# Two-layer block in fp32: lo parts of the attention's weights and of finished head-pair rows on Pool, and the second pair's rotations issued one per tick behind the urgent VectorE work

## The chip, the core and the metric

The kernel runs on one core of one Trainium2 chip. A core has a matrix engine (TensorE, "PE" in the profile, with its weight loads shown apart as "PEld"), a vector engine (VectorE, "DVE"), an activation engine (ScalarE, "ACT"), a general engine (GpSimd, "POOL") and an engine that issues DMA transfers (SyncE, "SP"). The metric is the device time of one execution in microseconds, as a median over runs.

## The reference, cut to what matters

The reference is a two-layer block on a [1, 1024, 1024] input in fp32. Layer 0 mixes by a gated MLP and a convolution, layer 1 by attention; each layer ends in a convolutional FFN, and a norm closes the whole. The change lies in the attention of layer 1, which is in short:

```python
h = rms_norm(x, odd_norm_g[j])
qkv = (h @ odd_w_qkv[j]).reshape(bn, s, 3, ATTN_HEADS, HEAD_DIM)   # 16 heads of 64
q = rotary(qkv[:, :, 0], pos)        # x1*cos - x2*sin, x2*cos + x1*sin
k = rotary(qkv[:, :, 1], pos)
v = qkv[:, :, 2]
o = dilated_attention(q, k, v)       # three (window, dilation) patterns,
                                     # merged by their log-sum-exps
x = x + o.reshape(bn, s, D_MODEL) @ odd_w_o[j]
```

## The kernel before, in words

**Exact products from two parts.** Every matrix operand is held as two fp32r numbers, a hi part and a lo part. The hi part is a cast, made by ACT (`hi_of`, L206 in the profile). The lo part is the original less its hi part, a subtraction (`lo_of`). All subtractions, additions and products of DVE and POOL go through one small recording class, so that in the profile they have one line, L138; they are told apart by engine and tile names. A projection is then three products (hi·hi, lo·hi, hi·lo; L268 to L270).

**The attention's stages.** The 16 heads are worked on as eight pairs, `hp` 0 to 7, each about 60 us long. In a pair there are 20 steps, each of two ticks. A step makes, on PE: the scores of a later query block (`pss`, L1482 and L1483), the transposes of exponentials made before (`ppt`, L1549 and L1550, in `turn`), and the product of transposed exponentials with the values (`po`, L1569, in `value`) for the step two steps back. Between PE's parts stand, for the scores, a masked maximum on DVE and an exponential on ACT; and, for the transposes, a cast to hi on ACT (tile `tt`), a subtraction to lo on DVE (tile `tt`, from `ppt` in PSUM), and on some steps a small POOL memset of the tile's unused corner.

**What is fed in between.** While one pair runs its steps, the next pair is prepared: `prepare(hp)` projects the keys (`rk`), the queries (`rq`) and the values (`rv`) of that pair, a unit at a time by `feed`. Each projection of keys or queries is then rotated (`rotate`): four SP transfers swap the halves of each head into a tile `sw` (L1352), DVE multiplies `sw` by the sine and `rk`/`rq` by the cosine and adds them, ACT casts the sum to a hi part `rh`, and DVE subtracts it to a lo part `rl`. SP transfers (L1378) then put hi and lo of one head into the stacked operands `k` and `st`. The ticks at which these five steps come are written in `ROTATE = (1, 6, 7, 8, 9, 10)`: swap 1 tick after the projection's end, the sine product after 6, and so on to the lo part after 10; the first pair, which has no steps to run beside it, uses `ROTATE_FIRST`.

**The weights.** `Weights` fetches [128 x 1024] weight rows ahead (SP, L231), casts hi on ACT, and one tick later (`lo_at`) subtracts for lo, on DVE unless `lo_eng` says otherwise. When the lo part is written, the next fetch is issued.

**The end of a pair.** `finish_pair` takes the reciprocal of the row sums, writes it to DRAM and reads it back broadcast over partitions (tile `r`), multiplies the output `o` by it on DVE, casts to hi on ACT (into `r`), and, `O_LOW` = 3 ticks after the product (8 in pair 6), subtracts for lo on DVE into `o`; two SP transfers bring both to DRAM (L1619). The output projection takes them from there: `O_GROUPS = ((0,1,2),(3,4),(5,6,7))`. The first group's projection is fed in between the steps of pair 7; it needs the residual rows `x`, which SP loads (L1651) when pair 7 has been prepared.

**What sets the order.** Each engine executes its instructions in program order. The program order is written by a ticker: `after(n, fn, late)` puts a function on the tick n ticks ahead, where functions are sorted by `late` (negative first); `tick()` runs those due now, and then the ticker's hooks. An instruction that waits for a transfer or for another engine therefore holds up everything that was written after it for its engine.

Of the kernel before, what the change touches and what calls it, by code (L numbers as in the profile page):

```python
# [12 lines left out]
F32R = mybir.dt.float32r  # L13
# [132 lines left out]
def block_kernel(ctx, tc, io, out):  # L146
# [58 lines left out]
    def hi_of(hi, src):  # L205
        nc.scalar.copy(hi, src)  # L206
# [1110 lines left out]
    def attention(x_dram, hT, then, late):  # L1317
# [4 lines left out]
        nc.gpsimd.dma_start(cos, io["cos"])  # L1322
        nc.gpsimd.dma_start(sin, io["sin"])
        sets = {}

        def project(raws, fins):
            ws = weights.take(4)
# [14 lines left out]
                return box[0]  # L1342
            return get

        def rotate(raw, fin_h, fin_l, at):
            st = {}

            def swap():
                st["sw"] = sw = stile(name="sw")
                for b in range(4):  # L1350
                    a = b ^ 1
                    nc.sync.dma_start(sw[32 * b:32 * b + 32, :],  # L1352
                                        raw()[32 * a:32 * a + 32, :])

            def m2():
                vec.tensor_tensor(st["sw"], st["sw"], sin, op=ALU.mult)

            def m1():
                vec.tensor_tensor(raw(), raw(), cos, op=ALU.mult)

            def add():
                vec.tensor_tensor(raw(), raw(), st["sw"], op=ALU.add)

            def hi():
                st["rh"] = stile(dt=F32R, name="rh")
                hi_of(st["rh"], raw())

            def lo():
                st["rl"] = stile(dt=F32R, name="rl")
                lo_of(st["rl"], raw(), st["rh"])  # L1370

            for n, fn in zip(at, (swap, m2, m1, add, hi, lo)):
                after(n, fn)
            after(at[-2] + 1, lambda: fin_h(st["rh"]), 1)
            after(at[-1] + 1, lambda: fin_l(st["rl"]))

        def stack(t, z, src, e):
            nc.sync.dma_start(f32v(t[z * HD:(z + 1) * HD, :]), f32v(src[e * HD:(e + 1) * HD, :]))  # L1378
# [1 line left out]
        def prepare(hp):  # L1380
# [51 lines left out]

            rk, rq, rv = lazy("rk"), lazy("rq"), lazy("rv")
            at = ROTATE if hp else ROTATE_FIRST
            fins = [lambda: rotate(rk, k_hi, k_lo, at), lambda: rotate(rq, q_hi, q_lo, at)]
            if hp:
                yield from project([rk], fins[:1])
                yield from project([rq], fins[1:])
# [145 lines left out]
        def finish_pair(hp):  # L1584

            o = outs_o.pop(hp)
            ls = lsum[hp]
            st = {}

            def a():  # L1590
                vec.reciprocal(ls, ls)

            def b():
                st["ps"] = bank("psl")
                nc.tensor.transpose(st["ps"][0:16, 0:P], ls, ident)

            def c():
                st["row"] = smpool.tile([16, P], F32, tag="lrow", name=nm("lrow"), bufs=1)
                nc.scalar.copy(st["row"], st["ps"][0:16, 0:P])
                nc.sync.dma_start(l_dram[hp], st["row"])  # L1600

            def d():
                st["r"] = r = stile(name="r")
                for e in range(2):
                    src = l_dram[hp, 8 * e:8 * e + 8, :].rearrange("a b -> (a b)")
                    nc.sync.dma_start(r[e * HD:(e + 1) * HD, :], src.partition_broadcast(HD))

            def f():
                vec.tensor_tensor(o, o, st["r"], op=ALU.mult)
                if hp == KT - 1:  # L1610
                    oh, ol = hpair([P, S], "o")
                    split(o, oh, ol)
                    o_acts[hp] = tok_view(oh, ol)
                    return

                def low():
                    lo_of(o.bitcast(F32R), o, st["r"])
                    for z, part in enumerate((st["r"], o)):
                        nc.sync.dma_start(o_dram[hp, z], part)  # L1619
                after(1, lambda: hi_of(st["r"].bitcast(F32R), o))  # L1620
                after(O_LOW if hp < KT - 2 else O_LOW_LAST, low)
            after(1, a)
            after(2, b)
            after(3, c)
            after(4, d)
            after(9, f)
# [13 lines left out]
        def all_units():  # L1640
            for hp in range(KT - 1):
                yield from prepare(hp)

            for n, _ in enumerate(prepare(KT - 1)):
                if 20 <= n < 20 + len(O_GROUPS[0]):
                    o_fetch(n - 20)
                yield
            xb = [htile([P, 2, D], F32, "x") for _ in range(2)]
            for i in range(NT):
                xs.append(xb[i // 2][:, i % 2, :] if i < 4 else stile(name="x"))  # L1650
                after(1, lambda i=i: nc.sync.dma_start(xs[i], x_dram[i * P:(i + 1) * P, :]))  # L1651
            while any(k not in o_acts for k in O_GROUPS[0]):
                yield "wait"
            yield from down_units([o_acts[k] for k in O_GROUPS[0]], weights.take(4, W_O_DELAY), xs)

        fill = all_units()
# [46 lines left out]
        for n, ks in enumerate(O_GROUPS[1:]):  # L1703
            tk.until(lambda: all(k in o_acts for k in ks))
            if ks is O_GROUPS[-1]:
                late()
            down_group([o_acts[k] for k in ks], weights.take(4), xs if n == 0 else xn,
                       then(xn) if ks is O_GROUPS[-1] else None, to=xn)
# [212 lines left out]
```

## Time and profile before

| | |
|---|---|
| median of 3 runs | 2214.24 us (2212.09, 2214.24, 2214.68) |
| the profiled execution's own time | 2212.54 us |
| its span in the profile | 2210.8 us |
| PE busy | 2174.6 us, 98% |
| DVE busy | 1618.0 us, 73% |
| ACT busy | 1096.3 us, 50% |
| POOL busy | 687.8 us, 31% |
| mean granted PE clock | 0.998 |

Times in the trace count from the span's start. The attention's projections and its eight pairs lie between about 1000 and 1520 us. A row of the timeline gives start, duration, engine, line, operation and tiles (output <- inputs), and, in brackets, the idle time before it and what ended that. A row of waits for PEld gives the total time that weight loads of that line waited for the named releaser, how often, and the longest. "PEld" waits are what delays PE in this kernel, since each product needs its weights first. The columns of a table by stretch are busy time and count of each engine in that stretch, then the granted PE clock, the DMA share and GB/s.

### The profile page before, as it was taken

To read this page: it belongs to the slowest core of one execution; us is meant where nothing else is said; L and a number is where in the kernel's file an instruction comes from. 1 tells how busy PE (TensorE), PEld (TensorE's weight loads), DVE (VectorE), ACT (ScalarE), POOL (GpSimd) and SP (SyncE) were. 2 spreads that over 40 slices of the span, in tenths; PEclk is the share of its full clock that TensorE was granted. 3 is DMA by queue.
4 is the path that set the end of the run, shared out by engine and by line. 5 is a ranking of instruction groups with operands and counts; after the bars stand their busy time and mean duration, and the time that the engine had idled before them with its cause. 6 is when DMAs were issued, how large, how long until landed. Compare 5 with 4: busy or idle time off the path is not lost.

```text
span 2210.8 us, 29238 instructions
## 1 busy us (share of the span) xinstructions
PE 2174.6 (98%) x10448; PEld 1819.9 (82%) x10448; DVE 1618.0 (73%) x2583; ACT 1096.3 (50%) x1667; POOL 687.8 (31%) x529
## 2 busy tenths in 40 slices
PE   6999999999999999999999999999999999999998
PEld 6888888888888888888888888888888888888886
DVE  6998769877777865555777777786797777778556
ACT  5345365444444445353556555554654444444532
POOL 1122033766666340040000000001466666653001
PEclk9999999999999999999999999999999999999999
DMA  5479422444434597356344545743234444349933
GB/s 184 105 149 181 168 86 72 146 164 157 171 138 168 181 365 285 141 181 155 92 113 118 134 118 131 215 167 107 77 124 163 166 157 172 136 159 347 362 133 116
DMA packets 140849, 359.47 MB, mean 163 GB/s; under 512 B 16672, under 2 KB 17056, under 8 KB 140704
## 3 DMA queue, kind: packets, MB, share of 16 engines
q1 hardware_dynamic: 134512, 335.15, 45.0%
q0 software_dynamic: 5040, 18.27, 4.4%
q10 hardware_dynamic: 1152, 4.19, 0.5%
q8 instruction: 82, 1.34, 0.2%
q14 instruction: 63, 0.52, 0.1%
HBM read 219.68 MB, written 104.31 MB: 147 GB/s over the span
## 4 chain that ended last, share of the span: by engine, by line
PE 79%; issue 9%; DVE 6%; ACT 2%; DMA 1%; POOL 1%; SPq 1%; DVEq 0%; POOLq 0%; ACTq 0%
PE psd L1261 10%; PE psb L1082 7%; PE psb L1085 7%; PE psb L1083 7%; PE psu L269 6%; PE psu L270 6%; PE psu L268 6%; PE psc L1083 3%; PE psc L1082 3%; PE psc L1085 3%; PE po L1569 3%; PE psa L1083 2%; PE psa L1082 2%; PE psa L1085 2%; PE psd L268 2%
## 5 line engine op out<-in xcount | busy, mean ns | idle before, releaser
L1261 PE MATMUL psd<-ab 128*128 128x512 f32 x1800 | 409.9, 389 | 0.0
L1261 PEld LDWEIGHTS psd<-ab 128*128 128x128 f32 x1800 | 337.6, 188 | 69.9
L268 PE MATMUL psu<-hTh,w 128*128 128x512 f32 (+1 forms) x592 | 236.4, 399 | 0.1
L270 PE MATMUL psu<-hTh,w 128*128 128x512 f32 (+1 forms) x592 | 229.0, 387 | 0.0
L269 PE MATMUL psu<-hTl,w 128*128 128x512 f32 (+1 forms) x592 | 228.7, 386 | 0.2 <-DVE hTl L138 0.2
L206 ACT CAST ab<-ab 128x1024 fp32r<-128x1024 f32 x150 | 156.0, 1051 | 139.3 <-PE psd L1261 52.6
L138 DVE TENSOR_TENSOR ab<-ab,ab 128x1024 fp32r<-128x1024 f32 x150 | 191.5, 1331 | 36.2 <-ACT ab L206 35.7
L138 DVE TENSOR_TENSOR x<-psd,x 128x512 f32<-128x512 f32 x152 | 101.7, 687 | 135.2 <-PE psd L1261 107.4
L138 POOL MEMSET tt<- 128x256 f32 x64 | 19.9, 312 | 490.1 <-PE ppt L1550 158.6
L138 POOL TENSOR_TENSOR y<-y,y 128x512 f32<-128x512 f32 x66 | 94.6, 1434 | 186.3 <-DMA act<-y 110.4
L1119 ACT COPY sn<-psb 128x512 f32<-128x512 f32 x120 | 70.4, 587 | 165.1 <-PE psb L1085 121.7
L206 ACT CAST tt<-ppt 128x512 fp32r<-128x512 f32 (+1 forms) x160 | 86.6, 542 | 102.6 <-PE ppt L1550 66.5
L138 DVE TENSOR_TENSOR tt<-ppt,tt 128x512 fp32r<-128x512 f32 (+1 forms) x160 | 101.2, 634 | 48.4 <-ACT tt L206 47.3
L270 PEld LDWEIGHTS psu<-hTh,w 128*128 128x128 f32 x592 | 111.8, 189 | 23.1
L269 PEld LDWEIGHTS psu<-hTl,w 128*128 128x128 f32 x592 | 112.3, 190 | 17.4 <-DVE hTl L138 0.6
L268 PEld LDWEIGHTS psu<-hTh,w 128*128 128x128 f32 x592 | 112.2, 190 | 17.2 <-ACT rv L1331 0.4
L138 POOL TENSOR_TENSOR sm<-sm,mhalf 128x1 f32<-128x1 f32 (+2 forms) x38 | 31.5, 829 | 293.8 <-DVE sm L138 293.8
L138 POOL TENSOR_TENSOR s<-wr 128x512 f32<-128x512 f32 x40 | 86.2, 2156 | 108.3 <-DVE psa L138 97.9
L1499 ACT ACTIVATE p<-p,sma 128x896 f32<-128x896 f32 (+7 forms) x128 | 99.5, 778 | 37.0 <-DVE sma L138 36.4
L138 DVE TENSOR_TENSOR wl<-wr,wh 128x1024 fp32r<-128x1024 f32 x88 | 117.3, 1333 | 0.5 <-ACT wh L206 0.5
L1569 PE MATMUL po<-tt,v 128*128 128x256 f32 x640 | 110.0, 292 | 5.2 <-DVE tt L138 4.9
L138 DVE TENSOR_TENSOR pse<-psc,sn 128x512 f32<-128x512 f32 x40 | 28.0, 699 | 117.9 <-ACT sn L1119 117.9
(251 smaller groups left out, 5845.2 us busy)
## 6 DMA issues: line engine op xcount, KB each, us to landing
wr<-in_w_up_dram SPq DMA_DIRECT2D x88, 512.0 KB, 4.3
ab<-act SPq DMA_DIRECT2D x154, 256.0 KB, 5.4
act<-y SPq DMA_DIRECT2D x66, 512.0 KB, 3.0
wq<-in_w_down_dram SPq DMA_DIRECT2D x44, 512.0 KB, 5.2
wt<-wq SPq DMA_DIRECT2D x44, 512.0 KB, 4.6
ab<-wt SPq DMA_DIRECT2D x88, 256.0 KB, 5.4
ab<-in_w_down_dram SPq DMA_DIRECT2D x66, 256.0 KB, 5.6
wr<-in_w_qkv_dram SPq DMA_DIRECT2D x24, 512.0 KB, 4.1
```

What stands on the lines that cost most here:

```text
L138: return fn(*args, **kw)
L206: nc.scalar.copy(hi, src)
L268: nc.tensor.matmul(out_ap, st[0], mv[0], start=first, stop=False)
L269: nc.tensor.matmul(out_ap, st[0], mv[1], start=False, stop=False)
L270: nc.tensor.matmul(out_ap, st[1], mv[0], start=False, stop=last)
L1082: nc.tensor.matmul(ps, st[0], mv[0], start=f, stop=False, skip_group_check=True)
L1083: nc.tensor.matmul(ps, st[0], mv[1], start=False, stop=False, skip_group_check=True)
L1085: nc.tensor.matmul(ps, st[1], mv[0], start=False, stop=e, skip_group_check=True)
L1119: nc.scalar.copy(self.sn[key], self.b)
L1261: nc.tensor.matmul(ps, a[:, c], b[:, HALF:D], start=first and k == 0, stop=last and k == 2, skip_group_check=True)
L1499: nc.scalar.activation(p, p, AF.Exp, bias=sm[:, 2:3], scale=0.125, accum_out=lsum[hp][:, c:c + 1])
L1569: nc.tensor.matmul(po[:, c], v2[:, kb, :], tt[:, z, 256 * n:256 * n + 256], start=(g == 0 and n == 0 and z == 0), stop=(g == j and n == 1 ...
```

## The change

Three things are written otherwise; what is computed is the same, and PE's order is the same.

1. From the preparation of pair 1 until the first group of the output projection, `weights.lo_eng` is POOL: the lo subtraction of 23 weight tiles moves from DVE to POOL.
2. The lo subtraction of finished output rows in pairs 0 to 6 moves from DVE to POOL: 7 instructions.
3. `rotate` gets a function `put`. For pair 1 it puts the sine product, the cosine product, the addition and the lo subtraction in a queue, `big`, from which a hook of the ticker takes one per tick, after the tick's own functions. For the other pairs `put` calls at once. The steps are chained: the cast to hi is set when the addition has been written, with `late` 1; the stacking follows the cast and the subtraction by one tick.

```diff
+        big = deque()
+
+        def big_step():
+            if big:
+                big.popleft()()
+        tk.hooks.append(big_step)
...
-        def rotate(raw, fin_h, fin_l, at):
+        def rotate(raw, fin_h, fin_l, at, put):
...
             def add():
                 vec.tensor_tensor(raw(), raw(), st["sw"], op=ALU.add)
+                after(at[4] - at[3], hi, 1)

             def hi():
                 st["rh"] = stile(dt=F32R, name="rh")
                 hi_of(st["rh"], raw())
+                after(1, lambda: fin_h(st["rh"]), 1)
+                after(at[5] - at[4], lambda: put(lo), -1)

             def lo():
                 st["rl"] = stile(dt=F32R, name="rl")
                 lo_of(st["rl"], raw(), st["rh"])
-
-            for n, fn in zip(at, (swap, m2, m1, add, hi, lo)):
-                after(n, fn)
-            after(at[-2] + 1, lambda: fin_h(st["rh"]), 1)
-            after(at[-1] + 1, lambda: fin_l(st["rl"]))
+                after(1, lambda: fin_l(st["rl"]))
+
+            after(at[0], swap)
+            for n, fn in zip(at[1:4], (m2, m1, add)):
+                after(n, lambda fn=fn: put(fn))
...
             at = ROTATE if hp else ROTATE_FIRST
-            fins = [lambda: rotate(rk, k_hi, k_lo, at), lambda: rotate(rq, q_hi, q_lo, at)]
+            put = big.append if hp == 1 else (lambda fn: fn())
+            fins = [lambda: rotate(rk, k_hi, k_lo, at, put),
+                    lambda: rotate(rq, q_hi, q_lo, at, put)]
+            if hp:
+                weights.lo_eng = pool
...
                 def low():
-                    lo_of(o.bitcast(F32R), o, st["r"])
+                    lo_of(o.bitcast(F32R), o, st["r"], pool)
...
             while any(k not in o_acts for k in O_GROUPS[0]):
                 yield "wait"
+            weights.lo_eng = None
             yield from down_units([o_acts[k] for k in O_GROUPS[0]], weights.take(4, W_O_DELAY), xs)
```

DVE's order while pair 1's queries are rotated (`sw` and `rq`; `tt` are the transposed exponentials of pair 0, `sma` and `p` its scores):

```order
 L138 TENSOR_SCALAR sma_8281<-sma_8281 128x1
-L138 TENSOR_TENSOR sw_8238<-sw_8238,sin_7730 128x1024
 L138 TENSOR_TENSOR tt_8297<-ppt_8296,tt_8297 128x512
 L138 ISA p_8280,sma_8315<-pss_8316,mask_7728 128x512
 L138 ISA sma_8315 128x1
 L138 TENSOR_SCALAR sma_8315<-sma_8315 128x1
-L138 TENSOR_TENSOR rq_8144<-rq_8144,cos_7729 128x1024
-L138 TENSOR_TENSOR rq_8144<-rq_8144,sw_8238 128x1024
+L138 TENSOR_TENSOR sw_8238<-sw_8238,sin_7730 128x1024
+L138 TENSOR_TENSOR rq_8143<-rq_8143,cos_7729 128x1024
 L138 TENSOR_TENSOR tt_8324<-ppt_8323,tt_8324 128x512
```

The sine product now stands behind a `tt` subtraction and a maximum, and the addition has left its place ahead of the next `tt` subtraction.

POOL's order at the end of pair 6 (`w` are weight tiles, `o` the finished rows of pair 6, `tt` the memsets of the steps):

```order
+L138 TENSOR_TENSOR w_12197<-wr_11557,w_12197 128x1024
+L138 TENSOR_TENSOR w_12265<-wr_11808,w_12265 128x1024
 L138 MEMSET tt_12308 128x2x128
 L138 MEMSET tt_12349 128x2x128
+L138 TENSOR_TENSOR w_12339<-wr_12006,w_12339 128x1024
+L138 TENSOR_TENSOR o_11726<-o_11726,r_12234 128x1024
 L138 MEMSET tt_12418 128x2x128
```

Four subtractions stand there now among the memsets. On DVE two of them stood between the queries' lo part `rl` and a `tt` subtraction:

```order
-L138 TENSOR_TENSOR rl_12367<-rq_12058,rh_12339 128x1024
-L138 TENSOR_TENSOR w_12341<-wr_12006,w_12341 128x1024
-L138 TENSOR_TENSOR o_11726<-o_11726,r_12234 128x1024
+L138 TENSOR_TENSOR rl_12367<-rq_12058,rh_12343 128x1024
 L138 TENSOR_TENSOR tt_12349<-ppt_12348,tt_12349 128x384
```

Now `tt_12349` follows `rl` directly. On SP, at the same place, the transfers of pair 6's rows to DRAM now stand ahead of the stacking of `st`, and the loads of `x` behind both, as before.

More of the change, by code (lines that the diff above doesn't have):

```diff
@@ L1705, in attention @@
             if ks is O_GROUPS[-1]:
+                assert not big
+                tk.hooks.remove(big_step)
                 late()
```

## The prediction

> **What bounds the kernel now.** I read first the page's engine shares, then busy time by stretch for the attention (about 1000 to 1520 us), then what the weight loads wait for there, and last the timelines around each wait.
>
> ```profile
> PE 2174.6 (98%) x10448; PEld 1819.9 (82%) x10448; DVE 1618.0 (73%) x2583; ACT 1096.3 (50%) x1667; POOL 687.8 (31%) x529
> ```
>
> PE is the bound of the whole; only gaps on PE can be won. By stretch (columns: span of the stretch, then PE, PEld, DVE, ACT, POOL, then the granted clock, the DMA share and GB/s):
>
> ```profile
> 1000.00:1080.00 80.00, 77.15 (x405) 64.39 (x404) 51.58 (x107) 36.89 (x73) 1.65 (x6) 1.00 0.54 132
> 1080.00:1420.00 340.00, 339.13 (x1978) 293.99 (x1977) 263.77 (x594) 199.87 (x407) 14.21 (x46) 1.00 0.49 126
> 1420.00:1445.00 25.00, 22.61 (x128) 19.37 (x127) 19.32 (x43) 13.92 (x28) 0.74 (x3) 0.93 1.02 376
> 1445.00:1520.00 75.00, 74.51 (x434) 64.53 (x433) 60.22 (x136) 38.16 (x77) 3.33 (x11) 1.00 0.36 123
> ```
>
> In 520 us PE is idle 2.85 + 0.87 + 2.39 + 0.49 = 6.6 us. That is the ceiling of any gain here, some 0.3% of the span. POOL is nearly idle: 20 us of 520. The waits, in rows for 1000 to 1520, then for 1033 to 1040, 1040 to 1062 (two), 1062 to 1080, 1080 to 1420, 1420 to 1445 and 1445 to 1520 (total, times, longest):
>
> ```profile
> PEld po L1569 <- DVE tt L138: 7.3, 10, 2.4
> ...
> PEld po L1569 <- DVE tt L138: 0.8, 1, 0.8
> ...
> PEld po L1569 <- DVE tt L138: 1.4, 2, 1.0
> PEld ppt L1550 <- DVE tt L138: 1.3, 1, 1.3
> ...
> PEld ppt L1549 <- DVE sma L138: 0.6, 1, 0.6
> ...
> PEld po L1569 <- DVE tt L138: 1.5, 3, 0.7
> ...
> PEld po L1569 <- DVE tt L138: 2.8, 2, 2.4
> ...
> PEld po L1569 <- DVE tt L138: 0.9, 2, 0.7
> ```
>
> Nearly all of it is one wait: the lo part of the transposed exponentials comes late from DVE. DVE is not short of time (264 of 340 us busy); the `tt` subtraction is late because something of no urgency is written ahead of it. So the change is worth what those waits are worth, place by place.
>
> **Part 1, the queries' rotation of pair 1 (1040 to 1062).**
>
> ```profile
> 1049.98 1.23 DVE L138 TENSOR_TENSOR sw<-sw,sin 128x1024 f32<-128x1024 f32 x1 [4.61 <-DMA sw<-rq]
> 1051.13 0.68 DVE L138 TENSOR_TENSOR tt<-ppt,tt 128x512 fp32r<-128x512 f32 x1
> 1052.52 1.22 DVE L138 TENSOR_TENSOR rq<-rq,cos 128x1024 f32<-128x1024 f32 x1
> 1053.77 1.23 DVE L138 TENSOR_TENSOR rq<-rq,sw 128x1024 f32<-128x1024 f32 x1
> 1054.91 0.68 DVE L138 TENSOR_TENSOR tt<-ppt,tt 128x512 fp32r<-128x512 f32 x1
> ```
>
> DVE stands 4.61 us at the sine product, waiting for the swap's transfers, with the `tt` subtraction behind it; then the cosine product and the addition hold up the next one. The waits on PE:
>
> ```profile
> 1051.86 0.42 PEld L1569 LDWEIGHTS po<-tt,v 128*128 128x128 f32 x3 [0.97 <-DVE tt L138]
> 1055.65 0.14 PEld L1550 LDWEIGHTS ppt<-ident,p 128*128 128x128 f32 x1 [1.29 <-DVE tt L138]
> ...
> 1051.86 0.62 PE L1569 MATMUL po<-tt,v 128*128 128x256 f32 x3 [0.66 <-DVE tt L138]
> 1055.65 0.33 PE L1550 MATMUL ppt<-ident,p 128*128 128x128 f32 x1 [0.88 <-DVE tt L138]
> ```
>
> After the change `tt` goes first at both places, so that the 4.61 us fall on work that nobody on PE waits for soon. Of 1.4 + 1.3 us nothing is left: 2.7 us of load waits. Load waits overstate what PE loses: for the two shown, PE's own idle is 0.66 + 0.88 = 1.54 of 2.26, a share of 0.68. PE's ends are modelled and the truth lies between 0.68 and 1; I take 0.85. The chance that the queue makes pair 1's `st` and `k` late is small: they are shifted by one or two ticks of about 1.5 us.
>
> **Part 2, weights' lo parts on POOL (1062 to 1080).** The 0.6 us there is a maximum of the scores behind a weight's subtraction; it goes, and nothing takes its place, since POOL has only 0.31-us memsets to do.
>
> **Part 3, the pairs' ends (1080 to 1420).** In the fourth, as an example:
>
> ```profile
> 1240.62 1.23 DVE L138 TENSOR_TENSOR rl<-rq,rh 128x1024 fp32r<-128x1024 f32 x1
> 1241.77 1.22 DVE L138 TENSOR_TENSOR o<-o,r 128x1024 fp32r<-128x1024 f32 x1
> 1242.90 0.55 DVE L138 TENSOR_TENSOR tt<-ppt,tt 128x384 fp32r<-128x384 f32 x1
> ```
>
> With the output's subtraction on POOL, `tt` comes 1.2 us sooner, more than any of the three waits there (longest 0.7): 1.5 us go. They stay in part if POOL's subtraction holds up `rl`, priced below; bounds 0.7 and 1.5.
>
> **Price of POOL beside DVE.** Rows of POOL's groups and of DVE's, then a stretch where both subtract:
>
> ```profile
> L138 POOL TENSOR_TENSOR w<-wr,w 128x1024 fp32r<-128x1024 f32 x2 | 4.7, 2349 | 0.8 <-ACT w L206 0.8
> ...
> L138 DVE TENSOR_TENSOR rl<-rq,rh 128x1024 fp32r<-128x1024 f32 x8 | 9.8, 1219 | 0.0
> ...
> 804.44 4.11 DVE L138 TENSOR_TENSOR ab<-ab,ab 128x1024 fp32r<-128x1024 f32 x2 [0.35 <-ACT ab L206]
> ...
> 805.32 4.39 POOL L138 TENSOR_TENSOR wq<-wq,wq 128x512 f32<-128x512 f32 x2
> ```
>
> The same subtraction is 2.35 us on POOL and 1.22 on DVE. Side by side, two of DVE's took 4.11 instead of 2.44 us: one of the two engines stands while the other works. A `tt` subtraction, fed from PSUM, is not of this kind; `rl`, the rotations and the weights' subtractions, with both inputs in SBUF, are. The Trainium skill ("SBUF — State Buffer", section "Who interferes with whom") says that a DVE instruction with two SBUF inputs and a GpSimd instruction that reads SBUF exclude each other, whoever issues first blocking the other wholly. The rows agree (4.11 against 2.44). By that rule the move is free only where POOL's 2.35 us do not fall on a two-input instruction that `tt` waits behind, and the sum below is made so; without it the 0.2 us of the next part would not be lost, and the sum would be 3.8.
>
> **Part 4, the start.** The first moved subtraction comes when pair 0 is still being prepared:
>
> ```profile
> 1010.50 1.05 ACT L206 CAST w<-wr 128x1024 fp32r<-128x1024 f32 x1
> ...
> 1011.14 1.22 DVE L138 TENSOR_TENSOR sw<-sw,sin 128x1024 f32<-128x1024 f32 x1
> 1012.39 1.23 DVE L138 TENSOR_TENSOR rq<-rq,sw 128x1024 f32<-128x1024 f32 x1
> ...
> 1018.65 0.46 SPq L1378 DMA_DIRECT2D st<-rl  x1
> ...
> 1021.78 0.47 PE L1482 MATMUL pss<-k,st 128*128 128x512 f32 x1
> ```
>
> Here PE waits at 1021.78 for `st`, whose transfer is issued when `rl` is made. POOL becomes ready at 1011.55, when the cast ends, gets its turn when `sw` ends at 1012.36, and then holds up the addition at 1012.39 by up to 2.35 us. Against that DVE loses a weight's subtraction (1.22 us) which stood ahead of `rl`. The addition, the cast and `rl` follow each other, so most of the 2.35 us reaches `rl`, less 1.22 and less the slack that the chain has now. From the order of the chain I get `rl` later by 0.2 us; bounds: 0.5 lost, 0.4 won (no collision). The wait of 0.8 us at 1033 to 1040 stands behind the lo part of pair 1's keys, which the change leaves ahead of it: 0 won, at most 0.8.
>
> **Part 5, the end of pair 6 (1420 to 1445).** The largest single wait, 2.4 us:
>
> ```profile
> 1424.04 1.22 DVE L138 TENSOR_TENSOR rl<-rq,rh 128x1024 fp32r<-128x1024 f32 x1
> 1425.18 1.22 DVE L138 TENSOR_TENSOR w<-wr,w 128x1024 fp32r<-128x1024 f32 x1
> 1426.31 1.22 DVE L138 TENSOR_TENSOR o<-o,r 128x1024 fp32r<-128x1024 f32 x1
> 1427.44 1.15 DVE L138 TENSOR_TENSOR tt<-ppt,tt 128x384 fp32r<-128x384 f32 x2
> ...
> 1430.33 5.23 SPq L1651 DMA_DIRECT2D x<-x_attn  x7
> ...
> 1437.77 0.69 DVE L138 TENSOR_TENSOR x<-psd,x 128x512 f32<-128x512 f32 x1 [2.16 <-PE po L1569]
> ```
>
> Two subtractions leave the way of `tt`: 2.4 us would go. But two things come after. Four of POOL's subtractions now lie in this corner, 4 x 2.35 = 9.4 us, and POOL's hold on the rotation and on `rl` can bring back up to 1.2. And the residual `x` is added on DVE at 1437.77, right ahead of a `tt` on which PE waits next (the second of the two waits, 2.8 less 2.4 = 0.4). The row names PE as the releaser; I read it as the landing of `x`, 7.4 us after its issue at 1430.33. `x` is loaded behind `o`'s transfers, which wait for POOL's 2.35 us instead of DVE's 1.22, while the DMA share is 1.02: the loads are bound by the transfers, not by PE. If PE comes 2 us sooner and `x` does not, PE stands at that `tt` for the difference. I take this stretch as 0.3 us lost in all: what is won at 1428 is lost at 1438, and a little more. Bounds: 1.5 lost, 2.4 won.
>
> **Sum.** (2.7 + 0.6 + 1.5) x 0.85 = 4.1, less 0.2 at the start, less 0.3 at the end: 3.6 us, with 0.9 us at 1445 to 1520 unchanged (no moved instruction stands ahead of it). The profiled execution's 2212.54 would become 2208.9. That execution lies 1.7 us below the median 2214.24 (the span accounts for 2210.8 of it, 1.7 lie around it and stay). From the median, 2210.6 us.
>
> **The rivals.** *More is won:* POOL's subtractions miss DVE's two-input work at the start, the 0.8 us at 1033 goes (0.7), and 2.4 us at 1428 stay won: 4.1 + 0.7 + 2.4 = 7.2, about 2207 us. For it: POOL stood idle for most of 500 us; against it: POOL's start at 1012.36 falls on the addition, and the DMA share of 1.02. Chance 0.17.
>
> *Less is won:* the queue only delays the sine product, which again heads DVE before the second `tt` (1.3 x 0.85 = 1.1 lost of part 1), or the end loses 1.5: 4.1 - 0.2 - 0.3 - 1.1 = 2.5 or 4.1 - 0.2 - 1.5 = 2.4, and less with 0.7 in part 3: 2212 us. For it: the swap's transfer still arrives at 1049.98, in either order. Against it: in the new order a maximum lies between. Chance 0.16.
>
> *Slower:* the exclusion, at every pair's end. POOL's cast-to-subtraction step starts just before DVE's `rl`; `rl` waits 2.35 us where it is spared 1.22, so that `tt` behind it comes 1.13 later than now. Three ends already stall and pay it all, four have some slack and pay about half: 3 x 1.13 + 4 x 0.56 = 5.6, and 2.35 at the start, against (2.7 + 0.6) x 0.85 = 2.8 won in parts 1 and 2: 5 lost, 2219 us. It decides where POOL's start lies less than about 1.2 us ahead of `rl`'s. For it: 804 us, where the two alternate. Against it: DVE now goes from `rl` (1240.62) to `o` (1241.77) at once, so `rl` is issued before the moved subtraction is due. The rule of the Trainium skill named above is this rival's ground. Chance 0.11.
>
> **How the numbers follow.** The forecast has 0.56; its own range is 2208.5 to 2212.5 (bounds of the factor, 3.3 to 4.8 for 4.1, and of start and end by about 1). Runs of this kernel lie 2.6 us apart, so that 0.2%, 4.4 us, is what can be told from no change. Faster by more (below 2209.8): a third of the forecast's cases and nearly all of the first rival's, 0.19 + 0.16 = 0.35. Slower by more (above 2218.7): half of the last rival's and a little for what I have not seen, 0.10. Within: 0.55. The range, 2205.5 to 2216, takes in both milder rivals and leaves out most of the last one.
>
> **What would show it.** Right: no `tt` wait over 0.3 us between 1040 and 1080, and the sine product of `rq` idle before it without a PE wait; the three waits at 1120, 1242 and 1364 gone; POOL at about 90 us busy from 1000 to 1520 (20 + 30 x 2.35); the addition at 1012.4 later by about 2 us and the first `pss` at about 1022. At the end the `tt` wait moves from 1428 to 1438. Wrong: DVE's `rl` rows at 2 to 3.5 us rather than 1.22 at the pairs' ends, with `tt` waits behind them (the slower rival); or no new wait at 1438 and 2.4 us kept (more is won).

## The result, and the profile after

| | before | changed |
|---|---|---|
| median of 22 runs | 2214.34 us | 2210.57 us |
| range | 2212.09 to 2215.93 | 2209.13 to 2212.20 |
| ratio, 95% interval | | 0.9986 (0.9981 to 0.9992) |
| profiled execution, its span | 2212.54, 2210.8 us | 2211.90, 2210.2 us |

The changed kernel is 3.1 us faster by the ratio (1.8 to 4.2 us by its interval), 3.8 us by the medians. The forecast was 2210.6 us, 3.6 us less.

One correction to what stands ahead of the prediction: the finished rows that are stored at the end of pair 6's steps (`o_11726`, `r_12234`) are those of pair 5. A pair is finished while the next one runs.

The page's engine shares of the changed kernel:

```profile
PE 2173.8 (98%) x10448; PEld 1819.7 (82%) x10448; DVE 1587.6 (72%) x2553; ACT 1095.9 (50%) x1667; POOL 759.1 (34%) x559
```

DVE has 30 us less to do, POOL 71 us more: the same 30 subtractions, and the price of POOL. Busy time by stretch, columns as before:

```profile
1000.00:1080.00 80.00, 79.15 (x417) 66.68 (x416) 50.33 (x106) 37.74 (x75) 12.07 (x10) 1.00 0.55 132
1080.00:1420.00 340.00, 340.00 (x1983) 294.90 (x1982) 243.22 (x569) 201.22 (x409) 69.00 (x68) 1.00 0.49 129
1420.00:1445.00 25.00, 20.63 (x119) 17.86 (x118) 16.91 (x45) 13.15 (x28) 6.61 (x5) 0.93 0.94 337
1445.00:1520.00 75.00, 74.51 (x434) 64.49 (x433) 58.10 (x131) 37.63 (x76) 5.53 (x11) 1.00 0.35 121
```

In the last row's stretch PE is as busy as before; from 1080 to 1420 PE has no gap left. In 1420 to 1445 PE now has 4.4 us of gaps where it had 2.4. What the weight loads wait for in 1000 to 1520:

```profile
PEld ppt L1562 <- DVE sma L138: 3.6, 1, 3.6
PEld po L1582 <- DVE tt L138: 3.0, 5, 1.1
...
PEld ppt L1563 <- DVE tt L138: 0.5, 1, 0.5
PEld psu L268 <- DVE tt L138: 0.3, 2, 0.2
```

The waits for `tt` went from 7.3 + 1.3 to 3.0 + 0.5 + 0.3 us, and a new wait of 3.6 us, for a maximum of the scores (`sma`), has come at the end of pair 6. Its place, on DVE, SP, POOL and PE:

```profile
1422.24 1.31 DVE L138 TENSOR_TENSOR rl<-rq,rh 128x1024 fp32r<-128x1024 f32 x1
1423.48 1.31 DVE L138 TENSOR_TENSOR tt<-ppt,tt 128x384 fp32r<-128x384 f32 x2
...
1432.67 0.56 DVE L138 CUSTOM_DVE_ANT_0 p<-pss,mask 128x384 f32<-128x384 f32 x1 [5.37 <-DMA st<-rh]
...
1435.43 0.69 DVE L138 TENSOR_TENSOR x<-psd,x 128x512 f32<-128x512 f32 x1 [0.18 <-DMA x<-x_attn]
```

```profile
1425.82 0.32 SPq L1632 DMA_DIRECT2D o_dram<-o  x1
1426.24 0.49 SPq L1387 DMA_DIRECT2D st<-rh  x1
...
1427.53 1.06 SPq L1387 DMA_DIRECT2D st<-rh  x1
```

```profile
1422.43 3.36 POOL L138 TENSOR_TENSOR o<-o,r 128x1024 fp32r<-128x1024 f32 x1
```

```profile
1433.29 0.47 PE L1562 MATMUL ppt<-ident,p 128*128 128x128 f32 x1 [3.44 <-DVE sma L138]
```

DVE is idle for 5.37 us ahead of a maximum that writes the tile `p`, until a copy of `rh` to `st` has landed. In the built program this `p` has the address that `rh` of pair 7's queries had before it: `rh` must be copied out before `p` may be written. The two copies of `rh` are issued at 1426.24 and 1427.53, since on SP they now stand behind the store of the finished rows, which waits for POOL's subtraction to end at 1425.79. In the kernel before they were issued at 1423.07 and 1425.88, ahead of that store.

The later issue is not the whole of it. Here are the second copy and the same maximum, before and then changed (the last number of a copy's row is the time from issue to landing in us):

```profile
st<-rh SPq DMA_DIRECT2D x1, 256.0 KB, 7.4
1433.13 0.56 DVE L138 CUSTOM_DVE_ANT_0 p<-pss,mask 128x384 f32<-128x384 f32 x1 [2.02 <-PE pv L1447]
```

```profile
st<-rh SPq DMA_DIRECT2D x1, 256.0 KB, 4.9
```

Before, the copy landed at 1433.3, after `p` had been begun at 1433.13, so that `p` did not wait for it. Changed, it landed at 1432.4, no later than before, and `p` waited. What is new is the buffer: in the built program of before this `p` follows the tile `rv`, and the buffer of `rh` goes to a tile of `x`. The reordering has changed which buffer `p` gets. By the built programs `p` follows `rh` in the changed kernel and in the runs below with the queue alone, pair 5's rows on DVE, 8 weights back, the first weight back and the earlier reads; these are the runs in which DVE waits there for `st<-rh`, and no other does. Why the builder of the program hands out the buffers so was not looked into.

**Place by place.** PE executes the same 10448 matmuls in the same order in every run below, so their starts can be compared one by one with the first profile of before. The table gives, for stretches of that profile, by how much PE gained on it (negative) or fell behind, in us.

| run | 1000–1030 | 1030–1062 | 1062–1080 | 1080–1424 | 1424–1445 | 1000–1520 |
|---|---|---|---|---|---|---|
| changed | 0.15 | -2.25 | -0.60 | -1.24 | 1.59 | -2.32 |
| changed, second profile | 0.22 | -2.28 | -0.60 | -1.26 | 1.53 | -2.39 |
| before, second profile | -0.04 | 0.51 | -0.03 | 0.10 | -0.37 | 0.19 |
| weights only | 0.93 | 0.13 | -0.60 | -0.38 | 2.06 | 2.19 |
| rows only | -0.03 | 0.14 | 0.01 | -1.25 | 0.25 | -0.80 |
| queue only | 0.18 | -3.73 | -0.52 | 0.87 | -0.33 | -3.50 |
| changed, `st` first | 0.14 | -2.38 | -0.59 | -1.25 | 1.52 | -2.55 |
| changed, pair 5's rows on DVE | 0.15 | -1.10 | -0.60 | -1.27 | 1.87 | -0.94 |
| changed, rows one tick later | 0.13 | -2.26 | -0.61 | -1.25 | 1.49 | -2.45 |
| changed, 8 weights back | -0.25 | -3.29 | -0.61 | -1.25 | 2.02 | -3.33 |
| changed, first weight back | 0.19 | -3.73 | -0.61 | -1.25 | 1.56 | -3.81 |
| all in the queue, no POOL | -0.26 | -3.12 | -0.61 | -0.10 | 2.05 | -2.03 |

The two profiles of before differ by up to 0.5 us in one stretch, and the run with pair 5's rows on DVE, whose instructions in 1030–1062 are those of the changed kernel, by 1.2 us from it there: the last two stacking copies held SP for 3.44 us instead of 2.47 in the second profile of the changed kernel, and the swap behind them came 1.1 us later. Differences of such a size between single rows say nothing.

### The profile page after: what moved, and what is told of

Its sections match the earlier page's. It is cut to its first block, busy times and chain, and to the rows that moved or that the text cites. A ratio compares the mean times of both kernels' runs of the same rounds, so it can differ in the third digit from the quotient of the medians.

```text
span 2210.2 us, 29242 instructions
## 1 busy us (share of the span) xinstructions
PE 2173.8 (98%) x10448; PEld 1819.7 (82%) x10448; DVE 1587.6 (72%) x2553; ACT 1095.9 (50%) x1667; POOL 759.1 (34%) x559
## 4 chain that ended last, share of the span: by engine, by line
PE 86%; DVE 5%; issue 3%; ACT 2%; DMA 2%; POOL 1%; SPq 1%; DVEq 0%; POOLq 0%; ACTq 0%
PE psd L1261 17%; PE psb L1085 7%; PE psb L1082 7%; PE psb L1083 7%; PE psu L270 6%; PE psu L268 6%; PE psu L269 6%; PE psc L1082 3%; PE psc L1083 3%; PE psc L1085 3%; PE po L1582 3%; PE psa L1082 2%; PE psa L1083 2%; PE psa L1085 2%; PE psd L268 2%
```

## The experiments

**Each part alone.** Part 1 alone (weights): the kernel before with two lines.

```diff
+            if hp:
+                weights.lo_eng = pool
...
+            weights.lo_eng = None
             yield from down_units([o_acts[k] for k in O_GROUPS[0]], weights.take(4, W_O_DELAY), xs)
```

> Only the weights' lo parts on POOL; rotations and output rows as before. Place by place: the 0.6 us wait of the scores at 1062 to 1080 goes, the 2.4 us wait at 1428 halves (one of the two subtractions behind rl leaves), the waits at 1040 to 1062 and the three at the pairs' ends stay, the addition at 1012 grows from 1.2 to about 3.3 us at a cost of 0.1 to 0.2 us on PE. The transfers of st stay ahead of those of the output rows, so no wait over 1 us on a maximum near 1433. In all 0.5 to 1.5 us less than before, about 2213. The rival that exclusion costs more than the saved DVE time expects no less time, or more, than before.

Measured: 2214.76 us, ratio 1.0003 (0.9993 to 1.0012): no gain that can be told. The wait at 1062 went as expected; the start cost 0.9 us, not 0.1 to 0.2, and the wait near 1428 did not halve but grew from 2.4 to 3.5 us. On DVE and POOL there:

```profile
1424.89 1.23 DVE L138 TENSOR_TENSOR rl<-rq,rh 128x1024 fp32r<-128x1024 f32 x1
1426.03 3.38 DVE L138 TENSOR_TENSOR o<-o,r 128x1024 fp32r<-128x1024 f32 x1
1429.33 1.14 DVE L138 TENSOR_TENSOR tt<-ppt,tt 128x384 fp32r<-128x384 f32 x2
```

```profile
1424.91 3.42 POOL L138 TENSOR_TENSOR w<-wr,w 128x1024 fp32r<-128x1024 f32 x1 [7.15 <-ACT w L206]
```

POOL is ready with DVE's `rl` at 1424.9, stands while DVE runs it, and then holds DVE's next subtraction, which takes 3.38 us instead of 1.22. So moving one of two adjacent subtractions to POOL made the other one dearer by more than was saved. The expectation of a gain was wrong, and the rival's was right.

Part 2 alone (output rows): one word, `lo_of(o.bitcast(F32R), o, st["r"], pool)`.

> Only the output rows' lo parts on POOL. Place by place: the waits at 1122, 1243 and 1364 go (1.4 to 1.5 us), 2.4 us at 1428 halves; the waits at 1040 to 1080 stay. SP's order is that of before (st, then the rows, then x), so that the rows' subtraction of 2.4 to 3.4 us delays x and not st: no long wait on a maximum at 1433, but more wait at 1438. In all 1 to 2 us less than before, about 2213. The rival that POOL's subtraction blocks rl expects rl of 2 us or more and waits of over 0.5 us at those three places.

Measured: 2212.65 us, ratio 0.9994 (0.9985 to 1.0004), so that the runs do not tell it from before; the profile is 0.80 us ahead from 1000 to 1520. The three pairs' ends won 1.25 us, nearly the 1.4 to 1.5 expected and as in the changed kernel. At the end of pair 6 comes the same collision, with the engines' parts exchanged; `tt` waits 3.3 us, where half of 2.4 was expected:

```profile
1422.53 1.22 DVE L138 TENSOR_TENSOR rl<-rq,rh 128x1024 fp32r<-128x1024 f32 x1
1423.66 3.39 DVE L138 TENSOR_TENSOR w<-wr,w 128x1024 fp32r<-128x1024 f32 x1
```

Part 3 alone (the queue and the chaining): the changed kernel's `rotate`, with all lo parts on DVE.

> Only the rotations' queue and chaining; all lo parts on DVE. Place by place: 1.8 us of the load waits at 1040 to 1062 go as in the changed kernel, those at the pairs' ends and at 1428 stay. SP's order at 1420 to 1430 is the new one, the output rows ahead of st. If that order is what makes the wait of 3.6 us on a maximum near 1433 (the tile of p takes rh's buffer, which is free when st is copied), a wait of 1 to 3 us stands there too. If POOL's long subtraction of the rows is needed for it, nothing over 0.5 us stands there. In all 0 to 1.5 us less than before by the first, 1.8 by the second.

Measured: 2210.36 us, ratio 0.9986 (0.9977 to 0.9995): as fast as the whole change. Pair 1 wins 3.7 us, more than the 1.8 expected and more than the 2.25 of the changed kernel. At the end the new order on SP alone makes a wait of the same kind, with nothing on POOL:

```profile
1424.02 0.32 SPq L1630 DMA_DIRECT2D o_dram<-o  x1
1424.44 0.49 SPq L1387 DMA_DIRECT2D st<-rh  x1
```

```profile
PEld ppt L1560 <- DVE sma L138: 1.8, 1, 1.8
```

It is half as long; DVE ends the rows at 1423.99 where POOL, in the changed kernel, ended them at 1425.79, and the second copy lands at 1431.1 instead of 1432.4. The 0.87 us lost from 1080 to 1424 come from a late `tt` at 1239.5 and two new waits for a maximum, of 0.6 us or less, near 1246 and 1368. Parts 1 and 2 together thus add nothing to part 3 that the runs can tell: by the profiles, what they win at the pairs' ends (0.87 to -1.24, 2.1 us) they pay in pair 1 (1.5) and at the end (1.9). Much of the 1.9 is PE's clock. The changed kernel has 3.01 us of PE's work at a granted clock of 0.50 (1432.89 to 1436.30), an estimated loss of 1.5 us; with the queue alone the clock is 1.00 throughout 1420 to 1445. For the same reason the queue alone is 0.33 us ahead of before there, though PE stands for 3.6 us (2.03 and 1.56) where it stood for 2.24.

**The order of the transfers at the end.** The changed kernel with `st` ahead of the rows again:

```diff
-                after(1, lambda: fin_l(st["rl"]))
+                after(1, lambda: fin_l(st["rl"]), -1)
```

> The changed kernel with one thing more: the transfers that stack st are put ahead of those of the output rows again. If their order makes the 3.6 us wait near 1433, it goes, and rh's buffer is free by about 1429. What then ends the stretch is x: its loads still stand behind the rows' transfers, which wait for POOL until 1425.8, so PE gets a new wait of 1 to 3.5 us at the first addition of x, near 1436. In all 0.5 to 2.5 us less than the changed kernel. If the order of st has no part in it, the wait near 1433 stays at 3 us or more.

Measured: 2211.70 us, ratio 0.9990 (0.9980 to 0.9999): no gain over the changed kernel. The wait for the maximum has gone, so the order of the copies made it, but not through their lateness alone. Here is the second copy of `rh`, issued at 1422.60, and the maximum:

```profile
st<-rh SPq DMA_DIRECT2D x1, 256.0 KB, 6.2
1426.02 0.56 DVE L138 CUSTOM_DVE_ANT_0 p<-pss,mask 128x384 f32<-128x384 f32 x1 [0.28 <-PE pv L1460]
```

`p` is begun 2.8 us before the copy lands: as in the kernel before, it follows `rv`, and `x` gets the buffer of `rh`. Order and buffer change together in every run, so that none shows what the later issue would cost by itself. In place of the wait, on ACT and on DVE:

```profile
1431.29 0.59 ACT L206 CAST tt<-ppt 128x512 fp32r<-128x512 f32 x1 [3.24 <-DMA o_dram<-r]
```

```profile
1433.65 0.69 DVE L138 TENSOR_TENSOR x<-psd,x 128x512 f32<-128x512 f32 x1 [5.15 <-DMA x<-x_attn]
```

First a `tt` waits for the buffer of `r`, which is being stored, then the addition waits for `x`. PE loses 1.52 us in the stretch instead of 1.59. That is the first forecast of the prediction's part 5, `x` as the limit, and it comes true only once the other wait is removed: the waits stand one behind the other.

**Pair 5's rows back on DVE**, one instruction of the changed kernel: `None if hp == KT - 3 else pool`.

> The changed kernel with one instruction back on DVE: the lo part of pair 5's output rows, the one at the end of pair 6. By the chain rows, st, rh's buffer, p: st is copied when the rows are made, about 1.2 us sooner than in the changed kernel (POOL took 3.4 us, DVE takes 1.2 behind rl, but may itself wait for POOL's weight subtraction), so the wait near 1433 shrinks by 1 to 2 us, and the wait near 1424 grows by about 1.2 us since the subtraction stands ahead of tt again. In all within 1 us of the changed kernel. If POOL's subtraction has no part in it, the wait near 1433 stays at 3.6 us.

Measured: 2209.27 us, ratio 0.9982 (0.9973 to 0.9992). The wait for the maximum is 2.4 instead of 3.6 us, that for `tt` 2.3 instead of 1.1: what one gave the other took, as expected. In this profile pair 1 won only 1.10 us, with the same instructions there as the changed kernel (the later swap named above), so its sum in the table says little.

**Rows one tick later**, `O_LOW = 4`, to bring POOL's subtraction onto `rl` at the pairs' ends.

> The changed kernel with the output rows' subtraction one tick later (O_LOW 4 for 3), which puts POOL's 2.4 us nearer to DVE's rl in the pairs whose ends stalled. The predicted rival says that a start of POOL less than 1.2 us ahead of rl costs tt more than was saved: rl of 2 to 3.4 us at the ends of pairs 2 to 5 and waits of 0.5 to 1.5 us each there, 2 to 5 us in all more than the changed kernel. If POOL starts behind rl instead, rl stays at 1.2 to 1.4 us and nothing is lost there. At the end the stacking comes ahead of the rows again by the later tick, so the wait near 1433 goes in either case and one on x takes its place.

Measured: 2211.03 us, ratio 0.9989 (0.9979 to 0.9999). The eight `rl` of the queries in groups by line from 1000 to 1520, the same row in the changed kernel and here, and then POOL's rows here:

```profile
L138 DVE TENSOR_TENSOR rl<-rq,rh 128x1024 fp32r<-128x1024 f32 x8 | 10.7, 1337 | 0.5 <-ACT rh L206 0.5
```

```profile
L138 POOL TENSOR_TENSOR o<-o,r 128x1024 fp32r<-128x1024 f32 x7 | 17.8, 2544 | 10.5 <-ACT r L206 10.5
```

Nothing was lost, but the run does not test the rival: POOL starts when ACT's cast is done, so that the later tick moves nothing. At the fourth `rl`, for one, it starts 2.05 us ahead in both runs (1176.13 and 1178.18 there, 1174.80 and 1176.85 here), and `rl` takes 1.44 us. At the end, as expected, the wait for the maximum went and DVE stood 5.26 us for `x`. The rival's condition, a start about 1.2 us ahead, came just once, in the run with 8 weights back at the end of pair 6:

```profile
1416.84 2.41 POOL L138 TENSOR_TENSOR o<-o,r 128x1024 fp32r<-128x1024 f32 x1 [6.39 <-ACT r L206]
1418.07 2.26 DVE L138 TENSOR_TENSOR rl<-rq,rh 128x1024 fp32r<-128x1024 f32 x1
```

POOL starts 1.23 us ahead of `rl`, and `rl` takes 1.0 us longer than alone. So the slower rival's mechanism is real, and its condition did not come at the other pairs' ends. That POOL can hold a two-input instruction of DVE for 2 us is shown by the runs with one part alone.

**Where pair 1 loses 1.5 us.** Two runs ask whether POOL's part in pair 1 is the cause. In the first, 8 of the 23 weight subtractions, those of pair 1 and those near the end, are back on DVE:

```diff
-                weights.lo_eng = pool
+                weights.lo_eng = pool if 2 <= hp < KT - 1 else None
```

> The changed kernel with the first three and the last five of the 23 weight subtractions back on DVE; the 15 between and the output rows stay on POOL. If the exclusion of POOL and DVE is what made pair 1 win less in the changed kernel (2.7 us to 1068) than with the queue alone (4.0), pair 1 wins 3.7 to 4.2 us here, the additions and products of the rotation there are all 1.2 us, and the waits at the pairs' ends are gone as well: 5 us ahead of before at 1400. At the end POOL's subtraction of the rows then falls on DVE's weight subtraction, which takes 3.4 us as in the run with the rows alone, with a wait of 2 to 3.3 us near 1425. In all 0.5 to 1.5 us less than the changed kernel. If the exclusion is not the cause, pair 1 wins 2.7 us as before.

Measured: 2207.66 us, ratio 0.9976 (0.9966 to 0.9987), the lowest median of all. From 1000 to 1080 it wins 4.15 us, where 3.7 to 4.2 were expected up to 1068, and at the pairs' ends 1.25. At the end POOL's rows fell on `rl`, shown above, and not on the weight's subtraction, which took 1.21 us; waits of 2.1 us for `tt` and 2.6 us for the maximum follow. The copies of `rh` were issued early here, at 1419.70 and 1421.28, but the second took 8.2 us to land. In the second run, one instruction alone is back on DVE, the first:

```diff
             def low():
-                lo_of(lo, raw, hi, self.lo_eng)
+                eng = self.lo_eng
+                if eng is not None and self.skip:
+                    self.skip -= 1
+                    eng = None
+                lo_of(lo, raw, hi, eng)
...
                 weights.lo_eng = pool
+                weights.skip = int(hp == 1)
```

> The changed kernel with one instruction back on DVE: the first weight subtraction, the one that POOL takes at 1011 and that makes DVE's addition of rq 3.3 us long. If that collision is what pair 1 still pays, the addition is 1.2 us, rl of rq is made near 1015.8 instead of 1017.4, and with it all that stands behind it on SP: the swap of rk is issued near 1024.0 instead of 1025.7, that of rq near 1042.7 instead of 1044.4. The wait of 0.6 us near 1037 goes and those of 0.5 and 0.4 us after 1050 shrink: 0.8 to 1.3 us more are won from 1000 to 1062 than in the changed kernel (2.1). From 1080 on nothing differs: 1.25 us at the pairs' ends, 1.6 us lost at the end. In all 0.5 to 1.3 us less than the changed kernel. If the other 22 subtractions on POOL are what costs in pair 1, the swaps stay at 1025.7 and 1044.4 and nothing is won.

Measured: 2208.94 us, ratio 0.9982 (0.9972 to 0.9991); the interval overlaps those of the changed kernel and of the run before it, so that the gain is read from the profiles. DVE and SP in the second profile of the changed kernel:

```profile
1012.34 3.30 DVE L138 TENSOR_TENSOR rq<-rq,sw 128x1024 f32<-128x1024 f32 x1
...
1017.42 1.23 DVE L138 TENSOR_TENSOR rl<-rq,rh 128x1024 fp32r<-128x1024 f32 x1 [0.52 <-ACT rh L206]
```

```profile
1025.75 3.69 SPq L1358 DMA_DIRECT2D sw<-rk  x4
...
1044.36 3.62 SPq L1358 DMA_DIRECT2D sw<-rq  x4
```

and with the one instruction back:

```profile
1012.20 1.23 DVE L138 TENSOR_TENSOR rq<-rq,sw 128x1024 f32<-128x1024 f32 x1
1014.60 1.22 DVE L138 TENSOR_TENSOR w<-wr,w 128x1024 fp32r<-128x1024 f32 x1
1015.73 1.22 DVE L138 TENSOR_TENSOR rl<-rq,rh 128x1024 fp32r<-128x1024 f32 x1
```

```profile
1024.02 3.73 SPq L1363 DMA_DIRECT2D sw<-rk  x4
1042.74 3.52 SPq L1363 DMA_DIRECT2D sw<-rq  x4
```

The addition is 2.1 us shorter, `rl` 1.7 us earlier even with the weight's subtraction ahead of it, both swaps on SP 1.6 to 1.7 us earlier, and PE wins 1.45 us more in 1030 to 1062; all else is as in the changed kernel. One collision of 2 us at the start is carried by the chain addition, cast, `rl`, copies, swap, rotation to PE 25 to 45 us later. The times of `rl` and the swaps came out as expected; PE won a little more than the 0.8 to 1.3 us expected, for all three waits went. The table bears it out beyond single profiles: the five that have this instruction on POOL along with the queue win 1.1 to 2.4 us in 1030–1062, the four that have it on DVE win 3.1 to 3.7.

**No POOL at all.** All lo parts and rotations go through the queue on DVE, and `st` is stacked first:

```diff
-                weights.lo_eng = pool
+                weights.put = big.append
...
-                after(self.lo_at, low)
+                after(self.lo_at, low if self.put is None else lambda: self.put(low))
...
-            put = big.append if hp == 1 else (lambda fn: fn())
+            put = big.append if hp else (lambda fn: fn())
...
-                    lo_of(o.bitcast(F32R), o, st["r"], pool)
+                    lo_of(o.bitcast(F32R), o, st["r"])
...
-                after(O_LOW if hp < KT - 2 else O_LOW_LAST, low)
+                after(O_LOW if hp < KT - 2 else O_LOW_LAST, lambda: big.append(low))
```

> No lo part on POOL at all: rotations of all pairs, the weights' and the output rows' lo parts go through the queue, one per tick behind the urgent work, and st is stacked ahead of the rows. If the order on DVE, and not DVE's load, is what delayed tt, this wins all that the three parts win and pays no exclusion: 4 us to 1068, 1.4 us more at the pairs' ends, and no wait over 1.2 us near 1425. The end then hangs on the transfers of rows and x, as with st first: 2 to 3 us are lost there. In all 3 to 5 us less than before, and 0 to 2 less than the changed kernel. If POOL's help is needed, waits of tt over 0.5 us appear in pairs 2 to 6, and it is slower than the changed kernel.

Measured: 2210.73 us, ratio 0.9987 (0.9978 to 0.9997): as fast as the changed kernel, without POOL. Pair 1 wins 3.1 us. The pairs' ends win only 0.10 us by 1424 where 1.4 were expected. The three waits of before have gone; 0.5 us is lost near 1180 to 1190 and 0.4 us after 1420. From 1075 to 1415 four waits for `tt` stand, of 0.3 us at most, so that the expectation's sign for a need of POOL, waits over 0.5 us, did not come. That the queue, one step per tick, comes late with a subtraction that `tt` then waits behind is likely but not shown. At the end it waits for `x` as `st` first did:

```profile
1435.85 0.69 DVE L138 TENSOR_TENSOR x<-psd,x 128x512 f32<-128x512 f32 x1 [4.47 <-DMA x<-x_attn]
```

**Fewer transfers at the end.** On top of the fastest run, the rows of pairs 0 to 2 are read back eight units earlier (12 for 20 in the condition of `o_fetch`).

> The run with 15 weight subtractions on POOL, and one number more: the rows of pairs 0 to 2 for the output projection are read back eight units earlier, before the keys' stacking of pair 7 rather than at 1411 to 1417. If the end is bound by the transfers that crowd there (3 MB of rows, 1 MB stored, 1 MB stacked, 4 MB of x), the copies of st land in 2 to 3 us rather than 4.3 and x lands sooner: the wait of 2.6 us on a maximum near 1430 shrinks to 1 or less, nothing of it comes back at x, and the whole is 1.5 to 3 us less than that run. If only the order of the copies counts, the wait stays at 2 us or more. If the tiles that the earlier reads need are not free, SP stands at them and the keys' stacking with it, and waits of PE appear at the start of pair 7.

Measured: 2210.65 us, ratio 0.9990 (0.9980 to 0.9999), slower than the run it was built on. Its third case came: PE stood for 4.2 us to 1418.6, on nothing that the profile names,

```profile
PEld ppt L1563 <- issue: 4.6, 1, 4.6
```

and lost 5.3 us by 1424; of this it regained 2.7 by 1445, where the wait for a maximum was gone. As PE came 6 us later to that place, the run does not tell whether fewer transfers or the later arrival removed it. What holds PE there was not settled.

**Each kernel profiled once more.**

> The kernel before, profiled once more, to see what of its waits differs between executions. If the waits are fixed by program order, PE's starts in the attention agree within 0.3 us of the first profile from 1000 to 1420, and only the end, which hangs on transfers, and single places outside the attention differ, by 1 to 2 us in all.

> The changed kernel, profiled once more. The waits of the first profile (3.6 us on a maximum near 1429, 1.1 us near 1423, three of 0.4 to 0.6 us in pair 1) stand again within 0.5 us; the 1.4 us that its first profile lost against the kernel before at 233 us, where nothing is changed, are not lost again.

Measured: 2212.41 and 2209.84 us. The changed kernel's waits stand again (3.6 and 1.1 us at the end; 0.6, 0.5 and 0.4 in pair 1), and the 1.4 us that its first profile lost at 233 us, where nothing is changed, is not lost again. The kernel before differs from its first profile by 0.51 us in pair 1, more than the 0.3 expected. The spans, 2210.7 and 2208.1 us, are 2.6 us apart.

## Why the prediction was right, and where it was not

The total was right to less than the interval is wide (3.6 forecast; 3.1, from 1.8 to 4.2). The traces, however, show 2.3 to 2.6 us, and the steps did not all hold: the places sum to 1.2 us less than forecast, which is about what part 5 lost beyond its 0.3. That the median fell on the forecast nonetheless is partly luck. The rest, up to about 1 us, lies in executions that were not profiled: before's two profiled executions, 2212.5 and 2212.4, are quicker than most of its runs. Where it lies was not settled.

Of the signs named, these came: the three waits at the pairs' ends went, POOL is busy for 93.2 us from 1000 to 1520 (about 90 forecast), and the addition at 1012 is 2.1 us longer. These did not: `tt` waits of 0.5 and 0.4 us stayed between 1040 and 1080, where none over 0.3 was to stay, and the `tt` wait of 1428 did not move to 1438.

On DVE in the changed kernel:

```profile
1051.96 1.23 DVE L138 TENSOR_TENSOR sw<-sw,sin 128x1024 f32<-128x1024 f32 x1 [1.60 <-DMA sw<-rq]
1053.10 1.22 DVE L138 TENSOR_TENSOR rq<-rq,cos 128x1024 f32<-128x1024 f32 x1
1054.24 0.69 DVE L138 TENSOR_TENSOR tt<-ppt,tt 128x512 fp32r<-128x512 f32 x1
```

The prediction's ceiling, 6.6 us, counted PE's idle time alone and left out the clock, which the row for 1420 to 1445 gives as 0.93. In the kernel before PE works for 3.41 us at half clock, right behind the gap at 1428:

```profile
1428.96:1432.37 3.41, 3.41 (x12) 2.92 (x11) 1.68 (x4) 0.75 (x2) 0.00 (x0) 0.50 1.03 246
```

By these figures, as an estimate, another 1.7 us could be won there. The changed kernel did not win them, since the clock falls at its gap at 1433 as well; the queue alone did.

- **Part 1 (2.7 x 0.85 = 2.3 us).** 2.1 measured between 1045 and 1062. The mechanism held at the first place: the first `tt` goes ahead of the sine product. At the second it held in part: by the rows above the second `tt` stands behind both products, which wait for the swap, so that 0.5 us of its 1.3 stayed, and 0.4 us stayed further on. With the swap 1.7 us earlier (first weight back) no wait was left from 1030 to 1062.
- **Part 2 (0.6 x 0.85 = 0.5 us).** 0.60 measured; the factor was too low here. It held in the runs with the weights on POOL, but POOL is not needed for it: the queue alone won 0.52, and the run without POOL 0.61.
- **Part 3 (1.3 us).** 1.25 measured, in the runs with the rows on POOL.
- **Part 4 (0.2 us lost, 0 won at 1033 to 1040).** 0.15 and 0.22 lost, 0.15 and 0.20 won. The numbers held, but the step hid a larger one: the new chaining puts ACT's cast of `rh` in another place, and by itself made `rl` 1.4 us earlier (1015.97 in the queue alone, 1017.40 before). The collision on POOL ate this (1017.42 in the second profile). I priced the collision against the order of before instead of against the order that the rest of the change makes, and so did not see that one instruction of 30 cost 1.5 us.
- **Part 5 (0.3 us lost, bounds 1.5 lost to 2.4 won).** 1.5 to 1.6 lost: this step failed, in size and in cause. I named `x` as what comes late next. The `tt` wait fell from 2.4 to 1.1, not to nothing, with `rl` still ahead of it. Then came a wait of 3.6 us that I had not listed, on `p`, for a buffer. I had looked, for the stacking of `st` that was moved behind the rows' stores on SP, at when `st` is first used (late), and not at its source `rh`: the new order gives its buffer to `p`, which is needed soon, and no longer to `x`. The clock, which had fallen behind the gap of 2.24 us before, fell again at the new gap of 3.44 us.
- **The rivals.** "More is won" fell with the end. "Less is won" named the right loss, 1.5 us at the end, by a wrong cause, and its other ground, the sine product ahead of the second `tt`, came in part (0.5 us of the wait). "Slower" did not come; its mechanism is real (3.38 and 3.39 us instead of 1.22 in the runs with one part alone), and in the run with the weights alone it took back all that was won, at the end of pair 6 and at the start rather than at every pair's end.

The Trainium skill's rule on DVE and GpSimd ("SBUF — State Buffer", section "Who interferes with whom") agrees with these rows: the second one to issue stands for the whole of the first. It speaks against the weights' lo parts on POOL more than I let it: the two runs with the lowest medians both take the subtraction that meets the addition at 1012 off POOL.

## What to carry to other kernels

When a transfer is moved in a queue, look at both of its ends: who needs what it writes, and which tile takes the buffer that it reads, for the move itself can hand that buffer to another tile. When work goes to an engine that can hold up the one it relieves, price each instruction at its own place, against the order that the whole change makes: here 22 of the 23 weight subtractions cost nothing that the profiles show up to 1424, one cost 1.5 us, and the waits that arose 25 us and more behind it did not show its name. Ask first whether a better order on the busy engine does as much: here the queue alone was as fast as the whole change. And where several waits end at nearly the same time, as at the end of pair 6, the removal of one is worth only the distance to the next: three different waits took turns there, and every run with the end's weights and rows on POOL lost 1.5 to 1.6 us there.

## What was not expected of the hardware

The clock that PE is granted fell after one short gap and not after another. In the kernel before, after 2.24 us of idle time, the products stand 0.42 us apart:

```profile
1428.06 0.63 PE L1569 MATMUL po<-tt,v 128*128 128x256 f32 x3 [2.24 <-DVE tt L138]
...
1430.02 0.63 PE L268 MATMUL psd<-w,o 128*128 128x512 f32 x1
1430.44 0.63 PE L269 MATMUL psd<-w,o 128*128 128x512 f32 x1
```

With the queue alone, after 2.03 us at the same place, 0.24 us apart:

```profile
1424.52 0.62 PE L1580 MATMUL po<-tt,v 128*128 128x256 f32 x3 [2.03 <-DVE tt L138]
...
1425.99 0.40 PE L268 MATMUL psd<-w,o 128*128 128x512 f32 x1
1426.23 0.40 PE L269 MATMUL psd<-w,o 128*128 128x512 f32 x1
```

In the changed kernel the fall comes at the end of the 3.44 us gap; the granted clock is 0.59 from 1433 to 1437. The length of the gap alone does not decide: after 2.31 us at 1436.7 in the run without POOL the clock stayed at 1.00, and after 2.20 us at 1432.6 in the run with pair 5's rows on DVE it fell to 0.50. Each fall at this place lasts 3.41 us (6.83 with the weights alone), an estimated loss of up to 1.7 us in 3.41; so a gap near 2 us may cost either 2 or nearly 4. The Trainium skill ("TensorE: Matmul & The Clock Gate", section "What's actually happening") gives an idle window of about 3.4 us for the fall; here 2.24 us were enough in one case, so that the measurement differs from that figure.
